# Gate and value products of a feed-forward block by seven half-size products (Strassen), in three parts instead of two

## The chip, the cores and the metric

The kernel runs on one core of one Trainium2 chip. The metric is the device time of one execution in microseconds (us). The core has five engines with a queue each: TensorE (PE in the profile; its weight loads are shown apart as PEld), VectorE (DVE), ScalarE (ACT), GpSimd (POOL) and SyncE (SP, which issues most DMAs here). Each engine works through its own queue in order, and an instruction that waits for a semaphore holds back all that stands behind it in that queue.

## The reference, cut to what matters

The kernel computes two transformer blocks on 512 tokens of width 1024, in fp32. The change lies in the feed-forward part of the first block only:

```python
h = rmsnorm(x, norm_ffn[layer])
x = x + (jax.nn.silu(h @ w_ffn_gate[layer]) * (h @ w_ffn_up[layer])) @ w_ffn_down[layer]
return rmsnorm(x, norm_final)          # D_MODEL = 1024, D_FF = 2816, SEQ = 512
```

`h @ w_ffn_gate` (gate) and `h @ w_ffn_up` (value) are two products of 512x1024 by 1024x2816. Everything before and after (an NSA and a GLA mixer before; MLA, sliding-window, FoX and again MLA layers after) is computed by code that the change leaves as it was.

## The kernel before, in words

Every fp32 operand of a matmul is split into two fp32r parts, high and low, by `split_into` (L213): ACT copies the source to the high part, DVE subtracts the high part from the source to get the low part. `mm3` (L270) then takes three matmuls for each pair of operands: high by high, low by high, high by low. Weights come by `wload` (L228): a raw tile `wr` of 128x1024 (pool `wraw`, 3 buffers) is filled by a DMA from SP's queue, and is then split into a pair `wh`, `wl` (pool `wpool`, 6 buffers of each).

The activations lie transposed, features on partitions, in `Ah` and `Al` (8 chunks of 128 features by 512 tokens). They are written by `to_feat` at the end of the stage before (`merge`), one block of 128 tokens at a time.

`ffn` (L866) works in two parts (`FF_PART` = 11 of the 22 chunks of 128 hidden units). In each part it goes over the chunks two at a time. For each chunk there are 24 matmuls of 512 columns for the gate (8 feature chunks by three) into one PSUM bank and 24 for the value into another. `silu2` (L284: a Tanh on ACT and a scalar_tensor_tensor on DVE), a multiply on DVE (L891) and a split (L892) leave the hidden chunk in `hdh`, `hdl`. The very first pair of chunks runs as two halves of 256 tokens, so that it can start before the last token blocks are there. At the end of a part `out_proj` (L395) multiplies the hidden chunks by the rows of `w_ffn_down`: for each of two halves of 512 output columns and four blocks of 128 tokens, 33 matmuls of 512 columns, and an epilogue that adds the result to the residual `X` (L896). After the last part, the epilogue also normalises each block (L900 to L905) and turns it round with `to_feat`.

The order of the instructions on each engine is not written out by hand. The tile framework's scheduler sets it when the program is built, from the order of the code, its own estimate of durations, and the buffers that the pools give out; on the chip the order is then fixed.

Of the kernel before, what the change touches and what calls it, by code (L numbers as in the profile page):

```python
# [29 lines left out]
GLA_LEVELS = (32, 16, 8, 4, 2, 1)  # L30
D_FF = 2816
FF_CHUNKS = D_FF // 128
FF_PART = FF_CHUNKS // 2

COL_Q = 0
COL_KV = 512
# [91 lines left out]
class Net:  # L128
# [210 lines left out]
    def after(self, later, earlier, how=mybir.DependencyClass.NoSync):  # L339
        self.tc.add_manual_dep(later, earlier.name, mybir.DependencyInfo(how, mybir.DependencyReason.DATA), reason="order")  # L340
# [489 lines left out]
    def merge(self, w, rooms, early, oa, ob, spare):  # L830
        nc, a, tc = self.nc, self.a, self.tc
        with ExitStack() as c1:
# [30 lines left out]

            self.out_proj(a["w_out"][0], Split([(0, KD, *mg)]), epilogue)

    def ffn(self):  # L866
        nc, a, tc = self.nc, self.a, self.tc
        with ExitStack() as c1:
            f1 = c1.enter_context(tc.tile_pool(name="f1", bufs=1))
            f2 = c1.enter_context(tc.tile_pool(name="f2", bufs=2))  # L870
            hd = [f1.tile([128, FF_PART, S], F32R, name=n) for n in ("hdh", "hdl")]
# [4 lines left out]
            for part in range(2):  # L876
                for m0 in range(0, FF_PART, 2):
                    n = min(2, FF_PART - m0) * 128
                    col = (part * FF_PART + m0) * 128
                    wgs, wus = self.w_cols(wg, col, n), self.w_cols(wu, col, n)  # L880
                    for t in range(n // 128):
                        halves = 2 if part == 0 and m0 == 0 else 1
                        for hf in range(halves):
                            tok = slice(hf * S // halves, (hf + 1) * S // halves)
                            pg, pu = self.pj(), self.pj()
                            pg, pu = pg[:, 0:S // halves], pu[:, 0:S // halves]
                            self.proj_feat(pg, wgs[t], self.act, tok=tok)
                            self.proj_feat(pu, wus[t], self.act, tok=tok)
                            s = f2.tile([128, S], F32, name="fs")[:, 0:S // halves]
                            self.silu2(s, pg)  # L890
                            nc.vector.tensor_tensor(out=s, in0=s, in1=pu, op=ALU.mult)  # L891
                            self.split_into(hd[0][:, m0 + t, tok], hd[1][:, m0 + t, tok], s)  # L892
# [432 lines left out]
```

## Time and profile before

| | |
|---|---|
| median of 3 runs | 1878.99 us (1877.96 to 1880.93) |
| the profiled execution | 1878.37 us, of which span 1876.6 us |
| PE busy | 1830.0 us, 98% of the span |
| DVE, ACT, POOL busy | 1149.9 us (61%), 873.6 us (47%), 156.7 us (8%) |
| mean granted TensorE clock | 0.996 of full speed |

The feed-forward block takes from about 477 to 860 us of the span. Its matmuls on the first pair of chunks end at 502, the first part's gate and value products at 602.5, its down products at 663. A matmul's busy time in the trace is longer than the distance from one matmul to the next, since they are pipelined: cost is read from start to start. The same holds in a smaller measure for DVE and ACT.

### The profile page before, as it was taken

What the parts mean: (1) busy time and instruction counts of PE and PEld (TensorE: products, weight loads), DVE (VectorE), ACT (ScalarE), POOL (GpSimd) and SP (SyncE); (2) the same over time, 40 slices, a digit from 0 to 9 for tenths busy, and PEclk for the clock granted to TensorE, in tenths of its full rate; (3) what the DMA queues carried; (4) which work ended last, traced back from release to release, by engine and by line L of the source; (5) the groups of instructions that cost most, each with busy time, mean ns of one, the idle gap of its engine ahead of it and who ended that gap; (6) DMA issues with size and microseconds to landing.
All of it is one profiled execution on the core that took longest, in us unless ns stands there. A gap on an engine that the chain in (4) does not pass through costs nothing.

```text
span 1876.6 us, 26623 instructions
## 1 busy us (share of the span) xinstructions
PE 1830.0 (98%) x9843; PEld 1491.2 (79%) x9843; DVE 1149.9 (61%) x2954; ACT 873.6 (47%) x1970; POOL 156.7 (8%) x213
## 2 busy tenths in 40 slices
PE   7999899999999999999999999999999999999997
PEld 6877687678888888889877788877888887988775
DVE  5564387754533243336878675566776666787866
ACT  4543246743322132224667535463566564366651
POOL 2211200000000000002000010251000000200001
PEclk9999899999999999999999999999999999999999
DMA  7322042042333143214221133221422322232111
GB/s 217 79 57 57 15 126 62 18 135 90 113 99 87 62 135 93 81 54 135 54 65 56 46 110 96 68 66 38 113 70 55 90 68 79 76 87 58 46 57 45
DMA packets 200781, 148.09 MB, mean 79 GB/s; under 512 B 8797, under 2 KB 178570, under 8 KB 200650
## 3 DMA queue, kind: packets, MB, share of 16 engines
q1 hardware_dynamic: 198858, 140.97, 26.0%
q0 software_dynamic: 1792, 5.42, 0.9%
q8 instruction: 77, 1.26, 0.3%
q14 instruction: 54, 0.44, 0.1%
HBM read 144.27 MB, written 2.10 MB: 78 GB/s over the span
## 4 chain that ended last, share of the span: by engine, by line
PE 81%; DVE 3%; ACT 2%; issue 1%; POOL 0%; DMA 0%; POOLq 0%; DVEq 0%; ACTq 0%
PE pj L273 22%; PE pj L274 22%; PE pj L275 22%; PE o L348 4%; PE t L335 3%; PE s L309 1%; PE s L274 1%; PE s L273 1%; PE s L275 1%; PE s L310 1%; PE t L370 1%; ACT pt L205 1%; PE t L1178 1%; PE s L1278 1%; PE s L1277 1%
## 5 line engine op out<-in xcount | busy, mean ns | idle before, releaser
L214 ACT ACTIVATE wh<-wr 128x1024 fp32r<-128x1024 f32 (+9 forms) x390 | 280.4, 749 | 461.1 <-PE pj L274 270.4
L215 DVE TENSOR_TENSOR wl<-wr,wh 128x1024 fp32r<-128x1024 f32 (+9 forms) x390 | 322.2, 849 | 225.4 <-ACT wh L214 223.0
L273 PE MATMUL pj<-Ah,wh 128*128 128x512 f32 (+1 forms) x1120 | 435.2, 389 | 1.3 <-DVE k4l L215 0.8
L274 PE MATMUL pj<-Al,wh 128*128 128x512 f32 (+1 forms) x1120 | 434.0, 388 | 0.0
L275 PE MATMUL pj<-Ah,wl 128*128 128x512 f32 (+1 forms) x1120 | 433.6, 388 | 0.0
L273 PEld LDWEIGHTS pj<-Ah,wh 128*128 128x128 f32 x1120 | 210.8, 188 | 45.4 <-PE s L275 1.6
L275 PEld LDWEIGHTS pj<-Ah,wl 128*128 128x128 f32 x1120 | 210.8, 188 | 44.3 <-issue 1.5
L274 PEld LDWEIGHTS pj<-Al,wh 128*128 128x128 f32 x1120 | 210.8, 188 | 42.4 <-issue 0.8
L273 PE MATMUL pj<-wh,Ah 128*128 128x512 f32 (+5 forms) x640 | 217.8, 341 | 4.7 <-ACT Ah L214 4.6
L274 PE MATMUL pj<-wl,Ah 128*128 128x512 f32 (+5 forms) x640 | 215.9, 338 | 0.0
L275 PE MATMUL pj<-wh,Al 128*128 128x512 f32 (+5 forms) x640 | 213.4, 338 | 2.0 <-DVE Al L215 1.9
L325 ACT ACTIVATE sp<-sp,nm 128x128 f32<-128x128 f32 (+3 forms) x256 | 142.7, 559 | 68.0 <-DVE nm L324 65.8
L205 ACT ACTIVATE pt<-t 128x512 f32<-128x512 f32 (+3 forms) x288 | 114.9, 445 | 114.4 <-PE t L335 74.8
L322 DVE CUSTOM_DVE_ANT_0 sp<-s,c_causal 128x128 f32<-128x128 f32 (+3 forms) x256 | 121.0, 486 | 62.8 <-PE s L275 23.5
L273 PEld LDWEIGHTS pj<-wh,Ah 128*128 128x128 f32 x640 | 120.5, 188 | 19.5 <-ACT Ah L214 7.1
L275 PEld LDWEIGHTS pj<-wh,Al 128*128 128x128 f32 x640 | 120.2, 188 | 14.0 <-DVE Al L215 3.0
L274 PEld LDWEIGHTS pj<-wl,Ah 128*128 128x128 f32 x640 | 120.7, 189 | 10.8 <-issue 0.2
L335 PE MATMUL t<-ident,sp 128*128 128x128 f32 x640 | 107.9, 277 | 4.9 <-ACT pt L205 4.8
L335 PEld LDWEIGHTS t<-ident,sp 128*128 128x128 f32 x640 | 77.3, 140 | 30.4 <-ACT pt L205 11.5
L329 DVE TENSOR_SCALAR sp<-sp,rc 128x128 f32<-128x128 f32 (+3 forms) x256 | 96.6, 383 | 5.0
L275 PE MATMUL pj<-wh,hdl 128*128 128x512 f32 x176 | 68.3, 389 | 0.0
L274 PE MATMUL pj<-wl,hdh 128*128 128x512 f32 x176 | 68.3, 390 | 0.0
(417 smaller groups left out, 2827.2 us busy)
## 6 DMA issues: line engine op xcount, KB each, us to landing
wr<-in_w_in_dram SPq DMA_DIRECT2D x34, 512.0 KB, 3.8
wr<-in_fox_w_in_dram SPq DMA_DIRECT2D x30, 512.0 KB, 4.2
wr<-in_w_ffn_gate_dram SPq DMA_DIRECT2D x22, 512.0 KB, 3.9
wr<-in_w_ffn_up_dram SPq DMA_DIRECT2D x22, 512.0 KB, 3.9
wr<-in_w_ffn_down_dram SPq DMA_DIRECT2D x20, 512.0 KB, 3.7
wr<-in_swa_w_in_dram SPq DMA_DIRECT2D x20, 512.0 KB, 4.3
wr<-in_mla_w_in_dram SPq DMA_DIRECT2D x16, 512.0 KB, 4.4
wr<-in_mla_w_out_dram SPq DMA_DIRECT2D x16, 512.0 KB, 3.8
```

What stands on the lines that cost most here:

```text
L205: return self.nc.scalar.activation(out, in_, AF.Copy, scale=1.0 if scale is None else scale)
L214: self.nc.scalar.activation(h, src, AF.Copy)
L215: self.nc.vector.tensor_tensor(out=l, in0=src, in1=h.bitcast(F32), op=ALU.subtract)
L273: self.nc.tensor.matmul(ps, lhsT=ah, rhs=bh, start=i == 0, stop=False)
L274: self.nc.tensor.matmul(ps, lhsT=ah, rhs=bl, start=False, stop=False)
L275: self.nc.tensor.matmul(ps, lhsT=al, rhs=bh, start=False, stop=i == n - 1)
L309: self.nc.tensor.matmul(ps, lhsT=q, rhs=kh, start=True, stop=False)
L322: nc.vector.tensor_tensor_reduce(out=v, in0=ps, in1=self.causal[:, S - n:S], scale=1.0, scalar=LOWEST, op0=ALU.add, op1=ALU.max, accum_out ...
L325: nc.scalar.activation(v, v, AF.Exp, bias=nm[:, g], accum_out=sm[:, g])
L329: nc.vector.tensor_scalar(v, v, rc[:, g], None, ALU.mult)
L335: nc.tensor.transpose(ps[:, (b - j) * 128:(b - j + 1) * 128], sp[:, POFF[b] + j * 128:POFF[b] + j * 128 + 128], self.ident)
L348: mm = self.nc.tensor.matmul(po[64 * i:64 * i + 64, j * 128:S], lhsT=value(j, i), rhs=pt[:, TOFF[j]:TOFF[j] + (NB - j) * 128], start=first ...
```

## The change

The first pair of chunks stays as it was, except that only its first chunk is run in halves. For the other 20 chunks, two chunks (256 hidden units) are taken together. The weights of such a pair are a 1024x256 matrix, cut into four blocks of 512x128 (b11, b21, b12, b22); the activations are cut into halves by feature and by token (a11, a12, a22, and a21). Gate and value each become one "group" of seven products (a Strassen-Winograd scheme): four sums of the activation blocks are made once (`half_sums`: s1 to s4), four sums of the weight blocks for each group on POOL (`sub`, in place in the raw tiles), and each of the seven products is 4 feature chunks by three matmuls of 256 columns, 84 matmuls in all. A bank `a` keeps adding up: it holds the first product, is copied out by ACT (`kept`), takes the second on top, is copied again, and so on. DVE adds the copies to other banks for the four quarters of the result.

A group needs four weight pairs instead of two: w0 (the raw first tile), w1 (half of the raw second tile), and, once POOL has made the sums, w3 (first tile) and w2 (second tile). The code interleaves the groups by generators: the first two products of a group, then the last two of the group before, then the middle three. The three parts have 8, 8 and 6 chunks, so the down product runs three times, with 24, 24 and 18 matmuls per block. The second raw tile comes from a pool of its own (`fr`, 2 buffers).

```diff
-FF_PART = FF_CHUNKS // 2
+FF_PARTS = (8, 8, 6)
...
+    def half_sums(self, pool, room):
...
+        for eng, f, k, tok in ((nc.vector, f11, lo, t0), (nc.gpsimd, f22, hi, t1), (nc.vector, f21, lo, t1), (nc.gpsimd, f12, hi, t0)):
+            eng.tensor_tensor(out=f, in0=q(self.Ah, k, tok).bitcast(F32), in1=q(self.Al, k, tok).bitcast(F32), op=ALU.add)
+        nc.gpsimd.tensor_tensor(out=f22, in0=f21, in1=f22, op=ALU.add)
+        nc.vector.tensor_tensor(out=f21, in0=f11, in1=f21, op=ALU.subtract)
+        nc.vector.tensor_tensor(out=f11, in0=f22, in1=f11, op=ALU.subtract)
+        nc.gpsimd.tensor_tensor(out=f12, in0=f12, in1=f11, op=ALU.subtract)
...
+    def halves_product(self, pool, raws, sums, w, n0, out):
+        nc = self.nc
+        v0 = self.wload(w, 0, KD, (n0, 128))
+        v1 = self.wload(w, 0, KD, (n0 + 128, 128), pool=raws)
+        b11, b21, b12, b22 = v0[:, 0:4], v0[:, 4:8], v1[:, 0:4], v1[:, 4:8]
+        w0 = self.wtile(KD, 128)
+        self.split_into(*w0, v0)
+        w1 = self.wtile(4, 128)
+        self.split_into(*w1, b22)
+        sub = lambda o, x, y, op=ALU.subtract: nc.gpsimd.tensor_tensor(out=o, in0=x, in1=y, op=op)
+        sub(b22, b22, b12)
+        sub(b12, b12, b11)
+        sub(b11, b11, b22, ALU.add)
+        sub(b21, b21, b11)
+        w3 = self.wtile(KD, 128)
+        self.split_into(*w3, v0)
+        w2 = self.wtile(KD, 128)
+        self.split_into(*w2, v1)
...
+        a, b, c = self.pj()[:, 0:256], self.pst()[:, 0:256], self.pss()[:, 0:256]
+        product(a, w0, 0, "a11", first=True)
+        p1 = kept(a)
+        product(b, w0, 4, "a12", first=True, last=True)
+        out(0, 0, p1, b)
+        yield
+        product(a, w3, 0, "s2")
+        u2 = kept(a)
+        product(c, w2, 0, "s1", first=True)
+        product(a, w2, 4, "s3")
+        u3 = kept(a)
+        out(1, 1, u3, c)
+        yield
+        product(c, w1, 0, "s4", last=True)
+        out(1, 0, u2, c)
+        product(a, w3, 4, "a22", last=True)
+        out(0, 1, a, None)
+        yield
...
+                    for group in pair(m, (k0 + m) * 128):
+                        next(group)
+                        if before is not None:
+                            next(before)
+                            next(before, None)
+                            if after is not None:
+                                after()
+                                after = None
+                        next(group)
+                        before = group
```

How the built programs stand is shown at three places, all in the middle of the stage (before: first part; after: second part). On DVE before, `wl` is the low part of a weight tile, `fs` a gate tile, `pj` a PSUM bank:

```order
L215 TENSOR_TENSOR wl_5003<-wr_5000,wh_5002 128x1024 [waits DMAHW1_49,PE_49,Activation_49]
L286 SCALAR_TENSOR_TENSOR fs_4858<-fs_4858,pj_4808 128x512 [waits Activation_49]
L891 TENSOR_TENSOR fs_4858<-fs_4858,pj_4809 128x512 [waits DVE_49,PE_49]
L215 TENSOR_TENSOR wl_5009<-wr_5006,wh_5008 128x1024 [waits DMAHW2_49,Activation_49]
L215 TENSOR_TENSOR hdl_4340<-fs_4858,hdh_4339 128x512 [waits Activation_49]
```

One period of DVE after, from the batch of four weight splits of one group to the next batch. 6231 and 6235 are w3 and w2 of a value group, made from the raw tiles 6214 and 6216; 6348 and 6352 are w0 and w1 of the group behind it, from 6343 and 6345; `fg` and `fu` are gate and value tiles, `part` a copy of bank `a`:

```order
L215 TENSOR_TENSOR wl_6231<-wr_6214,wh_6230 128x1024 [waits Activation_49]
L215 TENSOR_TENSOR wl_6235<-wr_6216,wh_6234 128x1024 [waits Activation_49]
L215 TENSOR_TENSOR wl_6348<-wr_6343,wh_6347 128x1024 [waits DMAHW4_49,Activation_49]
L215 TENSOR_TENSOR wl_6352<-wr_6345,wh_6351 128x512 [waits DMAHW7_49,Activation_49]
L1001 SCALAR_TENSOR_TENSOR fg_6083<-fu_6294,fg_6083 128x512 [waits Activation_49]
L1001 SCALAR_TENSOR_TENSOR fg_6084<-fu_6297,fg_6084 128x512 [waits Activation_49]
L993 TENSOR_TENSOR fu_6213<-part_6338,s_6240 128x256 [waits DVE_49,Activation_49]
L993 TENSOR_TENSOR fg_6341<-part_6382,t_6368 128x256 [waits PE_49,Activation_49]
L993 TENSOR_TENSOR fu_6213<-part_6312,s_6240 128x256 [waits PE_49]
L961 TENSOR_TENSOR fg_6084<-fg_6084,fu_6213 128x512 [waits DVE_49]
L215 TENSOR_TENSOR wl_6360<-wr_6343,wh_6359 128x1024 [waits Activation_49]
```

In place of one weight split at a time, with a wait for PE between them, DVE now has four in a row, and two groups are mixed in them: w3 and w2 of one group stand ahead of w0 and w1 of the next.

On ACT before, the high parts:

```order
L214 ACTIVATE wh_5002<-wr_5000 128x1024 [waits DMAHW1_49,PE_49]
L285 ACTIVATE fs_4858<-pj_4808 128x512 [waits PE_49,Activation_49]
L214 ACTIVATE wh_5008<-wr_5006 128x1024 [waits DMAHW2_49,PE_49]
L214 ACTIVATE hdh_4339<-fs_4858 128x512 [waits DVE_49]
L214 ACTIVATE wh_5014<-wr_5012 128x1024 [waits DMAHW3_49,PE_49]
```

and after, in the same period as DVE's above:

```order
L214 ACTIVATE wh_6230<-wr_6214 128x1024 [waits Pool_49]
L214 ACTIVATE wh_6234<-wr_6216 128x1024 [waits Activation_49]
L214 ACTIVATE wh_6347<-wr_6343 128x1024 [waits DMAHW4_49,PE_49,Activation_49]
L214 ACTIVATE wh_6351<-wr_6345 128x512 [waits DMAHW7_49,PE_49]
L205 ACTIVATE fg_6083<-pj_6109 128x256 [waits PE_49]
L205 ACTIVATE part_6312<-pj_6238 128x256 [waits PE_49]
L1000 ACTIVATE fu_6294<-fg_6083 128x512 [waits Activation_49]
L1000 ACTIVATE fu_6297<-fg_6084 128x512 [waits DVE_49]
L205 ACTIVATE part_6338<-pj_6238 128x256 [waits PE_49]
```

The first high part of a batch now waits for POOL, and behind it in the queue stand the high parts that the next group starts with.

On POOL before, there is nothing between the last block of the stage before and the final normalisation (these rows follow each other):

```order
L377 TENSOR_SCALAR rms_4310<-ss1_4308 128x1 [waits DVE_49]
L225 TENSOR_TENSOR rmso_4312<-rms_4310,mhalf_84 128x1 [waits Pool_49]
L222 DMA gf_4342<-in_norm_final_dram 128x1024 [waits DMAHW3_49,DMAHW4_49,DVE_49,DMAHW5_49,PE_49,Activation_49]
L377 TENSOR_SCALAR rms_6563<-ss1_6561 128x1 [waits DVE_49]
L225 TENSOR_TENSOR rmso_6565<-rms_6563,mhalf_84 128x1 [waits Pool_49]
```

and after, four sums for each of 20 groups (here the groups of the raw tiles 6085 and 6087, and the first of 6214 and 6216):

```order
L907 TENSOR_TENSOR wr_6087<-wr_6087 128x512 [waits DMAHW3_49,DVE_49]
L907 TENSOR_TENSOR wr_6087<-wr_6087,wr_6085 128x512 [waits DMAHW0_49,Pool_49]
L907 TENSOR_TENSOR wr_6085<-wr_6085,wr_6087 128x512 [waits Pool_49]
L907 TENSOR_TENSOR wr_6085<-wr_6085 128x512 [waits Pool_49]
L907 TENSOR_TENSOR wr_6216<-wr_6216 128x512 [waits DMAHW5_49,DVE_49]
```

The first of the four waits for DVE (the split of w1 from the same raw tile), and each of the others for the one ahead of it.

## Rows read from the trace of the kernel before

**Rows 1.** The page: span, and busy time of each engine.
```profile
span 1876.6 us, 26623 instructions
PE 1830.0 (98%) x9843; PEld 1491.2 (79%) x9843; DVE 1149.9 (61%) x2954; ACT 873.6 (47%) x1970; POOL 156.7 (8%) x213
```
**Rows 2.** Windows: stretch, length, busy PE, PEld, DVE, ACT, POOL; clock, DMA share, GB/s.
```profile
500.00:602.00 102.00, 102.00 (x450) 83.14 (x449) 40.07 (x47) 28.68 (x38) 0.00 (x0) 1.00 0.33 95
```
**Rows 3.** Waits of PE from 475 to 870: us in total, times, longest.
```profile
PE t L370 <- DVE Al L215: 0.4, 1, 0.4
```
**Rows 4.** Timeline of PE: start, duration, line, tiles, shape.
```profile
496.08 0.28 PE L273 MATMUL pj<-Ah,wh 128*128 128x256 f32 x1
...
498.93 0.28 PE L273 MATMUL pj<-Ah,wh 128*128 128x256 f32 x1
...
502.14 0.40 PE L273 MATMUL pj<-Ah,wh 128*128 128x512 f32 x1
...
602.52 0.40 PE L273 MATMUL pj<-wh,hdh 128*128 128x512 f32 x1
```
**Rows 5.** Groups by line and shape, 475 to 870: count, busy, mean ns.
```profile
L215 DVE TENSOR_TENSOR wl<-wr,wh 128x1024 fp32r<-128x1024 f32 x61 | 74.7, 1226 | 98.8 <-ACT wh L214 98.2
L891 DVE TENSOR_TENSOR fs<-fs,pj 128x512 f32<-128x512 f32 x20 | 13.7, 687 | 55.6 <-PE pj L275 55.6
L215 DVE TENSOR_TENSOR hdl<-fs,hdh 128x512 fp32r<-128x512 f32 x20 | 13.7, 685 | 0.2
L215 DVE TENSOR_TENSOR wl<-wr,wh 128x512 fp32r<-128x512 f32 x4 | 2.7, 685 | 0.0
L214 ACT ACTIVATE wh<-wr 128x1024 fp32r<-128x1024 f32 x60 | 63.6, 1061 | 216.6 <-PE pj L274 148.4 <-PE pj L275 43.6 <-DMA wr<-in_w_ffn_down_dram 8.3
```
**Rows 6.** Timeline of ACT, then DVE, in the stage: weight splits and their followers.
```profile
518.84 1.06 ACT L214 ACTIVATE wh<-wr 128x1024 fp32r<-128x1024 f32 x1 [4.00 <-PE pj L274]
519.81 0.58 ACT L285 ACTIVATE fs<-pj 128x512 f32<-128x512 f32 x1
...
519.93 1.23 DVE L215 TENSOR_TENSOR wl<-wr,wh 128x1024 fp32r<-128x1024 f32 x1 [3.76 <-ACT wh L214]
...
525.50 1.22 DVE L215 TENSOR_TENSOR wl<-wr,wh 128x1024 fp32r<-128x1024 f32 x1 [0.18 <-ACT wh L214]
526.65 0.69 DVE L215 TENSOR_TENSOR hdl<-fs,hdh 128x512 fp32r<-128x512 f32 x1
```
**Rows 7.** POOL's two-input operations, by line: count, duration ns min/median/max.
```profile
L419 POOL TENSOR_TENSOR xg<-X,nm x2: 2385/2392/2398, 12.3 to 19.5; 128x1024 f32<-128x1024 f32 x2
L621 POOL TENSOR_TENSOR f<-gk,f x24: 460/572/1483, 64.9 to 210.1; 128x128 f32<-128x128 f32 x24
L612 POOL TENSOR_TENSOR f<-cum x24: 612/625/1432, 60.9 to 208.0; 128x256 f32<-128x256 f32 x24
```
**Rows 8.** Timeline of POOL, then DVE, 11 to 23 us.
```profile
12.32 2.40 POOL L419 TENSOR_TENSOR xg<-X,nm 128x1024 f32<-128x1024 f32 x1 [5.98 <-DMA X<-in_x_dram]
...
17.58 0.28 POOL L377 TENSOR_SCALAR rms<-ss 128x1 f32<-128x1 f32 x1
17.94 0.55 POOL L225 TENSOR_TENSOR rmso<-rms,mhalf 128x1 f32<-128x1 f32 x1
...
11.82 0.68 DVE L215 TENSOR_TENSOR Al<-t,Ah 128x512 fp32r<-128x512 f32 x1
12.43 2.92 DVE L215 TENSOR_TENSOR wl<-wr,wh 128x592 fp32r<-128x592 f32 x1
```
**Rows 9.** Timeline of POOL, then DVE, near 65 us.
```profile
64.87 1.48 POOL L621 TENSOR_TENSOR f<-gk,f 128x128 f32<-128x128 f32 x1 [1.81 <-ACT wh L214]
...
64.82 1.22 DVE L215 TENSOR_TENSOR wl<-wr,wh 128x1024 fp32r<-128x1024 f32 x1
```
**Rows 10.** Timeline of DVE, then POOL, near 1162 us.
```profile
1161.69 0.18 DVE L1165 RECIPROCAL sum<-sum 128x4 f32<-128x4 f32 x1
...
1162.05 0.94 POOL L1169 TENSOR_SCALAR sp<-sp,sum 128x256 f32<-128x256 f32 x1 [3.31 <-DVE sum L1165]
```

More of the change, by code (lines that the diff above doesn't have):

```diff
@@ L225, in power_half, with wload @@
         self.nc.gpsimd.tensor_tensor(out=out, in0=var, in1=self.mhalf[:, 0:n], op=ALU.pow)
-    def wload(self, w, k0, kc, *ranges):
+    def wload(self, w, k0, kc, *ranges, pool=None):
         n = sum(r[1] for r in ranges)
-        t = self.wraw.tile([128, 1024], F32, name="wr")
+        t = (self.wraw if pool is None else pool).tile([128, 1024], F32, name="wr")
         v = t[:, 0:kc * n].rearrange("p (k n) -> p k n", n=n)
@@ L864, in merge, with splits @@
             self.out_proj(a["w_out"][0], Split([(0, KD, *mg)]), epilogue)
+    def half_sums(self, pool, room):
+        nc = self.nc
+        lo, hi, t0, t1 = slice(0, 4), slice(4, 8), slice(0, 256), slice(256, 512)
+        q = lambda t, k, tok: t[:, k, tok]
+        f11, f21, f12, f22 = (room.tile([128, 4, 256], F32, name=n) for n in ("f11", "f21", "f12", "f22"))
+        for eng, f, k, tok in ((nc.vector, f11, lo, t0), (nc.gpsimd, f22, hi, t1), (nc.vector, f21, lo, t1), (nc.gpsimd, f12, hi, t0)):
[4 more added lines that the diff above has]
+        nc.gpsimd.tensor_tensor(out=f12, in0=f12, in1=f11, op=ALU.subtract)
+        out = {"a11": (q(self.Ah, lo, t0), q(self.Al, lo, t0)), "a12": (q(self.Ah, hi, t0), q(self.Al, hi, t0)), "a22": (q(self.Ah, hi, t1), q(self.Al, hi, t1))}
+        def splits():
+            for n, src in (("s2", f11), ("s3", f21), ("s1", f22), ("s4", f12)):
+                if n == "s1":
+                    h, l = q(self.Ah, lo, t1), q(self.Al, lo, t1)
+                else:
+                    h, l = (pool.tile([128, 4, 256], F32R, name=n + u) for u in "hl")
+                self.split_into(h, l, src)
+                out[n] = (h, l)
+            return out
+        return splits
@@ new lines, in halves_product, with product, kept @@
+    def halves_product(self, pool, raws, sums, w, n0, out):
+        nc = self.nc
+        v0 = self.wload(w, 0, KD, (n0, 128))
[14 more added lines that the diff above has]
+        self.split_into(*w2, v1)
+        def product(ps, wt, k0, name, first=False, last=False):
+            sh, sl = sums[name]
+            for k in range(4):
+                (ah, al), (bh, bl) = (wt[0][:, k0 + k], wt[1][:, k0 + k]), (sh[:, k], sl[:, k])
+                for i, (x, y) in enumerate(((ah, bh), (ah, bl), (al, bh))):
+                    nc.tensor.matmul(ps, lhsT=x, rhs=y, start=first and k == 0 and i == 0, stop=last and k == 3 and i == 2, skip_group_check=True)
+        def kept(ps):
+            t = pool.tile([128, 256], F32, name="part", bufs=4)
+            self.acopy(t, ps)
+            return t
+        a, b, c = self.pj()[:, 0:256], self.pst()[:, 0:256], self.pss()[:, 0:256]
[16 more added lines that the diff above has]
+        yield
@@ L869, in ffn @@
             f1 = c1.enter_context(tc.tile_pool(name="f1", bufs=1))
-            f2 = c1.enter_context(tc.tile_pool(name="f2", bufs=2))
-            hd = [f1.tile([128, FF_PART, S], F32R, name=n) for n in ("hdh", "hdl")]
+            raws = c1.enter_context(tc.tile_pool(name="fr", bufs=2))
+            most = max(FF_PARTS)
+            hd = [f1.tile([128, most, S], F32R, name=n) for n in ("hdh", "hdl")]
             st = f1.tile([128, NB, 2], F32, name="fss")
@@ L875, in ffn, with hidden @@
             wg, wu = a["w_ffn_gate"][0], a["w_ffn_up"][0]
[L876 to L892, printed above, removed]
+            def hidden(m, s, u, tok=slice(0, S)):
+                nc.vector.tensor_tensor(out=s, in0=s, in1=u, op=ALU.mult)
+                self.split_into(hd[0][:, m, tok], hd[1][:, m, tok], s)
@@ new lines, in ffn @@
+            with tc.tile_pool(name="f0", bufs=1) as f0:
+                splits = self.half_sums(f1, f0)
+                wgs, wus = self.w_cols(wg, 0), self.w_cols(wu, 0)
+                for t in range(2):
+                    halves = 2 - t
+                    for hf in range(halves):
+                        n = S // halves
+                        tok = slice(hf * n, (hf + 1) * n)
+                        pg, pu = self.pj()[:, 0:n], self.pj()[:, 0:n]
+                        self.proj_feat(pg, wgs[t], self.act, tok=tok)
+                        self.proj_feat(pu, wus[t], self.act, tok=tok)
+                        s = f0.tile([128, S], F32, name="fg", bufs=2)[:, 0:n]
+                        self.silu2(s, pg)
+                        hidden(t, s, pu, tok)
+                sums = splits()
@@ new lines, in ffn, with pair, add, out @@
+            f2 = c1.enter_context(tc.tile_pool(name="f2", bufs=2))
+            def pair(m, col):
+                g = [f2.tile([128, S], F32, name="fg", bufs=4) for _ in range(2)]
+                u = []
+                def add(tiles):
+                    def out(t, half, x, y):
+                        o = tiles[t][:, half * 256:half * 256 + 256]
+                        if y is None:
+                            self.acopy(o, x)
+                        else:
+                            nc.vector.tensor_tensor(out=o, in0=x, in1=y, op=ALU.add)
+                    return out
+                def gates():
+                    yield from self.halves_product(f2, raws, sums, wg, col, add(g))
+                    for t in g:
+                        th = f2.tile([128, S], F32, name="fu", bufs=3)
+                        nc.scalar.activation(th, t, AF.Tanh, scale=0.5)
+                        nc.vector.scalar_tensor_tensor(out=t, in0=th, scalar=1.0, in1=t, op0=ALU.add, op1=ALU.mult)
+                def ups():
+                    u.extend(f2.tile([128, S], F32, name="fu", bufs=3) for _ in range(2))
+                    yield from self.halves_product(f2, raws, sums, wu, col, add(u))
+                    for t in range(2):
+                        hidden(m + t, g[t], u[t])
+                return gates(), ups()
@@ L894, in epilogue, with down @@
+            def down(part, k0, n):
                 def epilogue(b, half, ps):
@@ L896, in epilogue @@
                     nc.vector.scalar_tensor_tensor(out=xv, in0=ps, scalar=0.5, in1=xv, op0=ALU.mult, op1=ALU.add)
-                    if part == 0:
+                    if part < len(FF_PARTS) - 1:
                         return
@@ L906, in epilogue @@
                         self.to_feat(self.X[:, b], b)
-                self.out_proj(a["w_ffn_down"][0], Split([(0, FF_PART, *hd)]), epilogue, kc=FF_PART, k0=part * FF_PART)
+                self.out_proj(a["w_ffn_down"][0], Split([(0, n, *hd)]), epilogue, kc=n, k0=k0)
+            k0, before, after = 0, None, None
+            for part, n in enumerate(FF_PARTS):
+                for m in range(0, n, 2):
+                    if part == 0 and m == 0:
+                        continue
+                    for group in pair(m, (k0 + m) * 128):
[8 more added lines that the diff above has]
+                        before = group
+                after = lambda part=part, k0=k0, n=n: down(part, k0, n)
+                k0 += n
+            next(before)
+            next(before, None)
+            after()
     def finish_layer(self, i, w, og, last):
```

## The prediction

> **What bounds the kernel now.** I read the page first: PE is busy for 98% of the span, the next engine, DVE, for 61% [rows 1]. Then the windows: from 500 to 602 us, the first part's gate and value products, PE is busy all the time at full clock, DVE for 40 of 102 us, ACT for 29, POOL not at all [rows 2]. Then PE's waits: the longest in the whole feed-forward stage is 0.4 us [rows 3]. So PE alone sets the time there, and what it costs is the number of matmuls times the distance from start to start. For 512 columns that is (602.52 - 502.14) / 432 = 0.2324 us (9 chunks of 48 matmuls), for 256 columns (498.93 - 496.08) / 24 = 0.1188 us [rows 4]: half the columns cost 51%.
>
> **What PE saves.** The 20 chunks had 960 matmuls of 512 columns, 223.1 us. They now have 20 groups of 84 of 256 columns: 1680 x 0.1188 = 199.6 us, 9.98 us a group. In the first pair, 96 matmuls of 256 become 48 of 512: -0.2 us. The down products keep 528 matmuls. If PE stays the bound, that is -23.7 us.
>
> **Whether the other engines can feed it.** Per group DVE has three splits of 1024 columns and one of 512, 3 x 1.23 + 0.69 = 4.4 us, plus three additions of 256 columns and two to four operations of 512; ACT has the high parts and four copies. Both stay below 10 us, and a count of busy time would call the change covered. But the order rows show a closed loop. ACT's high part of w3 waits for POOL's fourth sum. On DVE the low parts of w3 and w2 of this group stand ahead of those of w0 and w1 of the next. POOL's first sum for the next group waits for that w1, and the next group's w3 waits for POOL's fourth. Every group goes once round this loop, whatever PE does. I time it from the start of the high part of w3:
>
> - DVE starts on the low part 1.09 us later (518.84 to 519.93) and starts the next operation 1.15 us after a split of 1024 (525.50 to 526.65) [rows 6]. Low parts of w3, w2, w0, w1 start at 1.09, 2.24, 3.39 and 4.54; the last one, of 512 columns, takes 0.69 [rows 5] and ends at 5.23. ACT, with 0.97 us from start to start [rows 6], keeps ahead.
> - POOL starts 0.18 us behind DVE (1161.87 to 1162.05) [rows 10], at 5.41.
> - A sum of two tiles of 128x512 on POOL isn't in the trace. The same operation took 2.39 us for 128x1024 and at least 0.46 for 128x128 [rows 7]; the straight line gives 1.29. The lower end is 0.92, from 0.61 for 128x256 (there the second input is one column repeated) and that 0.46; the upper end is 1.34, with the 0.28 of an operation on one column [rows 8] as the fixed part ((2.39 - 0.28) / 2 + 0.28). I take 1.29, since both inputs are whole tiles as in the 1024 row. Four of them with 0.08 between (17.86 to 17.94) [rows 8] are 5.40: done at 10.81.
>
> So the loop takes 10.81 us with nothing in its way, 0.83 more than PE's 9.98. The cover that the sums seem to have, a whole group of PE time, is not there.
>
> [...] The rows allow 0.92 to 1.34. [...]
>
> **POOL and DVE hold each other up.** At 12.43 DVE's split of 592 columns took 2.92 us, although 512 take 0.69: POOL's multiplication ran from 12.32 to 14.72, and DVE ended 0.63 later [rows 5, 8]. The other way round, POOL's 128x128 took 1.48 instead of 0.46 when DVE's split had started 0.05 ahead of it [rows 7, 9]. Whoever is second waits for the whole of the other. In the loop, while POOL makes its sums, DVE has two-input operations on SBUF tiles: two scalar_tensor_tensor in the period in which a gate group ends, and the product and two low parts of the hidden chunks where a value group ends (L961, then L215 twice). I let them take turns. DVE's first follows 0.61 after w1's start (11.82 to 12.43 for 512 columns) [rows 8], at 5.15, and ends at 5.83, so POOL starts at 5.83 instead of 5.41.
>
> - Gate: sum to 7.12, DVE to 7.80, sum to 9.09, two more with 0.08 ahead of each: 11.83.
> - Value: sum to 7.13, DVE to 7.81, sum to 9.10, DVE to 9.79, sum to 11.08, sum to 12.45.
>
> Mean 12.14 us, 2.16 more than PE needs. Bounds: 0.83 more with no such clashes; none at all, if a sum takes 0.92 and nothing clashes (loop 9.33). From above, about 3.2, if a clash costs one more wait in each period.
>
> **How often.** Parts have 6, 8 and 6 groups. Behind a down product the sums of the first group are done, so the loop is paid 5 + 7 + 5 = 17 times: 17 x 2.16 = 36.7 us. At each start of a part PE has two products (2.85 us) in hand while ACT copies bank a and makes the high parts of w3 and w2, 0.97 apart; the order puts two matmuls of w2 behind two of w3, so PE stands about 0.8 us, three times: 2.4.
>
> **The rest.** Half sums: POOL has three operations of 2.39 and eight sums of 1.29 to make after the last token block, 17.5 us, and DVE some eleven two-input operations of 1.15 at the same time, 12.7; PE has about 16 us of the first pair and 5.7 of first products (48 matmuls) to cover them. Were they to exclude each other fully, some 30 - 22 = 8 us would show; half of that and a little, 5 (0 to 10). The third down product adds eight additions to X on DVE and no matmul; the row splits of each down product now meet the last group's batch. One split (1.15) each, 3 us (0 to 6). Weight traffic is the same; SP's loads wait for buffers that come free a group ahead.
>
> **Sum**, against the profiled execution's own 1878.4 us (span 1876.6 [rows 1] and 1.8 around it; the median is 1879.0): -23.7 + 36.7 + 2.4 + 5 + 3 = +23.4: 1902 us. Its own range, with the last two terms at either end and 0.3 us on the period: 1889 to 1915.
>
> **Rivals.**
> - *The loop turns, but cheaper.* Either the clashes do not add up, since POOL slips between DVE's operations (10.81): -23.7 + 14.1 + 10.4 = +0.8, 1879; or a sum takes 0.92 and they do (10.66): 1877. For it: DVE's two-input operations fill only 1.4 to 2 us of a period. Against it: both rows of a clash show the full wait. 16%.
> - *PE stays the bound, faster.* Place: the queue of the high parts on ACT. If a sum takes under 1.08 us and nothing clashes, w3 is ready before PE asks, and only the opening is paid: -23.7 + 5 = 1860. It decides at a period of 9.98; the whole change breaks even at 9.98 + 13.3 / 17 = 10.76, with clashes a sum of 0.95. For it: the 0.61 row; PE's order has other products to fill in. Against it: the 2.39 row. 19%.
> - *A second wait inside the group.* Bank a is copied by ACT between products that PE adds to it; where the copy stands behind a Tanh or a high part, PE stands too. At 1 us for each of 17 periods that does not fall into the loop's slack: 1919. Against it: 12 to 20 matmuls lie between. 10%.
> - That the matmuls do not fall to 1680 is ruled out by the order.
>
> **Chances.** The forecast has 55%. What a measurement can tell from no change is about 0.2%, 3.8 us. Faster: the 19% and a quarter of the first rival, 23%. Same: half of that rival, 8%. Slower: the rest, 69%. The range runs from the PE-bound rival to the upper end of the forecast, 1859 to 1916; beyond lie the second wait and the worst of the opening.
>
> **What would show it.** In the profile after: POOL's sums on wr at 1.29 us or up to 2 where DVE is in the way; in the middle of a part PE idle some 2 us per group, waiting for ACT wh (w3) released by POOL; groups 12 us apart; POOL busy for about half of the stage; 256-column matmuls still 0.119 apart. A PE without gaps in the groups, or sums under 1 us, would make the forecast wrong; sums held up by DVE in no row would cut it to no change.

## The result, and the profile after

The changed kernel takes 1895.29 us (median of 4 runs, 1895.15 to 1895.97) against 1878.94 us: ratio 1.0086, 95% interval 1.0071 to 1.0101. The prediction was 1902 us (1859 to 1916).

The page of the changed kernel, answering to [rows 1], with the head of its chain of waits:

```profile
span 1893.3 us, 28314 instructions
...
PE 1821.4 (96%) x10515; PEld 1511.5 (80%) x10515; DVE 1253.8 (66%) x3065; ACT 933.6 (49%) x2090; POOL 285.7 (15%) x297
...
PE 51%; issue 12%; POOL 7%; DVE 2%; ACT 1%; POOLq 0%; DVEq 0%; ACTq 0%
PE pj L273 13%; PE pj L274 13%; PE pj L275 13%; POOL wr L907 6%; PE o L348 3%; PE t L335 3%; PE s L274 1%; PE s L273 1%; PE s L275 1%; PE t L370 1%; PE t L1318 1%; PE s L1418 1%; PE s L1417 1%; PE o L1273 1%; PE s L309 0%
```

POOL, busy for 15% of the span, has 7% of the chain, nearly all of it in the sums (L907). The window over the second part's groups, answering to [rows 2] (same columns):

```profile
629.00:727.00 98.00, 89.64 (x683) 84.02 (x682) 69.58 (x82) 48.81 (x81) 47.28 (x32) 1.00 0.32 95
```

PE, full in [rows 2], has gaps; every other engine is idle for a quarter of the time or more. Such a picture asks for a closed chain of waits. The two largest waits of POOL and ACT from 640 to 720 us (total, times, longest):

```profile
POOL wr L907 <- DVE wl L215: 38.3, 7, 5.6
ACT wh L214 <- POOL wr L907: 21.3, 7, 3.2
```

One round of it, in the timelines of POOL (first four rows; a row is one batch, the four sums of a group), ACT, DVE and PE, and then the durations (ns, least, median, most) of the gate's scalar_tensor_tensor (L1001) and, from 583 us on, of the low parts of the hidden chunks:

```profile
629.42 5.40 POOL L907 TENSOR_TENSOR wr<-wr 128x512 f32<-128x512 f32 x4 [49.68 <-DVE wl L215]
640.36 6.11 POOL L907 TENSOR_TENSOR wr<-wr 128x512 f32<-128x512 f32 x4 [5.53 <-DVE wl L215]
652.09 6.45 POOL L907 TENSOR_TENSOR wr<-wr 128x512 f32<-128x512 f32 x4 [5.62 <-DVE wl L215]
663.83 6.11 POOL L907 TENSOR_TENSOR wr<-wr 128x512 f32<-128x512 f32 x4 [5.30 <-DVE wl L215]
...
658.57 3.48 ACT L214 ACTIVATE wh<-wr 128x1024 fp32r<-128x1024 f32 x4 [3.21 <-POOL wr L907]
669.98 2.95 ACT L214 ACTIVATE wh<-wr 128x1024 fp32r<-128x1024 f32 x3 [2.93 <-POOL wr L907]
...
652.53 3.48 DVE L215 TENSOR_TENSOR hdl<-fg,hdh 128x512 fp32r<-128x512 f32 x2
659.65 4.10 DVE L215 TENSOR_TENSOR wl<-wr,wh 128x1024 fp32r<-128x1024 f32 x4 [0.55 <-ACT wh L214]
663.67 2.38 DVE L1001 SCALAR_TENSOR_TENSOR fg<-fu,fg 128x512 f32<-128x512 f32 x2
...
659.67 0.38 PE L922 MATMUL pj<-s2h,wh 128*128 128x256 f32 x1 [0.80 <-ACT wh L214]
660.62 0.39 PE L922 MATMUL s<-Ah,wh 128*128 128x256 f32 x1 [0.45 <-ACT wh L214]
...
L1001 DVE SCALAR_TENSOR_TENSOR fg<-fu,fg x20: 681/1020/1782, 526.2 to 825.4; 128x512 f32<-128x512 f32 x20
L215 DVE TENSOR_TENSOR hdl<-fg,hdh x16: 683/1772/1785, 586.3 to 837.8; 128x512 fp32r<-128x512 f32 x16
```

At 658.57 ACT starts the high part of w3, 0.03 us after POOL's last sum. DVE's four low parts begin 1.08 later and end at 663.75; POOL starts 0.08 behind, and ACT starts the next group's w3 at 669.98. From batch to batch (the period) it is 11.73 and 11.74 us; PE's 84 matmuls need 9.98. The first batch of a part meets nothing on DVE and takes 5.40, four sums of 1.29 with 0.08 between. Later ones take 6.11 where the two scalar_tensor_tensor of a gate fall into them, 6.45 where the hidden chunks do. Those DVE operations take longer too: of a gate's two the first, which starts ahead of the batch, takes 0.68 and the second 1.78, and each low part of a hidden chunk 1.78.

### The profile page after: what moved, and what is told of

Same layout as the page of the kernel before. It is cut to its first block, busy times and chain, and to the rows that moved or that the text cites. A ratio compares the mean times of both kernels' runs of the same rounds, so it can differ in the third digit from the quotient of the medians.

```text
span 1893.3 us, 28314 instructions
## 1 busy us (share of the span) xinstructions
PE 1821.4 (96%) x10515; PEld 1511.5 (80%) x10515; DVE 1253.8 (66%) x3065; ACT 933.6 (49%) x2090; POOL 285.7 (15%) x297
## 4 chain that ended last, share of the span: by engine, by line
PE 51%; issue 12%; POOL 7%; DVE 2%; ACT 1%; POOLq 0%; DVEq 0%; ACTq 0%
PE pj L273 13%; PE pj L274 13%; PE pj L275 13%; POOL wr L907 6%; PE o L348 3%; PE t L335 3%; PE s L274 1%; PE s L273 1%; PE s L275 1%; PE t L370 1%; PE t L1318 1%; PE s L1418 1%; PE s L1417 1%; PE o L1273 1%; PE s L309 0%
## 5 line engine op out<-in xcount | busy, mean ns | idle before, releaser
L214 ACT ACTIVATE wh<-wr 128x1024 fp32r<-128x1024 f32 (+10 forms) x428 | 307.2, 758 | 329.6 <-PE pj L274 108.3
L215 DVE TENSOR_TENSOR wl<-wr,wh 128x1024 fp32r<-128x1024 f32 (+10 forms) x428 | 357.3, 865 | 156.2 <-ACT wh L214 152.8
L273 PE MATMUL pj<-Ah,wh 128*128 128x512 f32 (+1 forms) x784 | 306.3, 391 | 2.3 <-DVE fg L286 1.0
L274 PE MATMUL pj<-Al,wh 128*128 128x512 f32 (+1 forms) x784 | 305.1, 389 | 0.2 <-DVE Al L215 0.2
L275 PE MATMUL pj<-Ah,wl 128*128 128x512 f32 (+1 forms) x784 | 304.6, 389 | 0.0
L273 PEld LDWEIGHTS pj<-Ah,wh 128*128 128x128 f32 x784 | 147.6, 188 | 32.9 <-PE s L275 1.6
L275 PEld LDWEIGHTS pj<-Ah,wl 128*128 128x128 f32 x784 | 147.6, 188 | 30.5 <-issue 1.5
L274 PEld LDWEIGHTS pj<-Al,wh 128*128 128x128 f32 x784 | 147.6, 188 | 29.3 <-issue 0.8
L322 DVE CUSTOM_DVE_ANT_0 sp<-s,c_causal 128x128 f32<-128x128 f32 (+3 forms) x256 | 120.8, 486 | 63.0 <-PE s L275 23.5
L907 POOL TENSOR_TENSOR wr<-wr 128x512 f32<-128x512 f32 x80 | 119.3, 1491 | 202.7 <-DVE wl L215 198.1
L274 PEld LDWEIGHTS pj<-wl,Ah 128*128 128x128 f32 x640 | 120.7, 189 | 10.8 <-issue 0.2
```

Of the source, the lines that this page charges most:

```text
L214: self.nc.scalar.activation(h, src, AF.Copy)
L215: self.nc.vector.tensor_tensor(out=l, in0=src, in1=h.bitcast(F32), op=ALU.subtract)
L273: self.nc.tensor.matmul(ps, lhsT=ah, rhs=bh, start=i == 0, stop=False)
L274: self.nc.tensor.matmul(ps, lhsT=ah, rhs=bl, start=False, stop=False)
L275: self.nc.tensor.matmul(ps, lhsT=al, rhs=bh, start=False, stop=i == n - 1)
L322: nc.vector.tensor_tensor_reduce(out=v, in0=ps, in1=self.causal[:, S - n:S], scale=1.0, scalar=LOWEST, op0=ALU.add, op1=ALU.max, accum_out ...
```

## Experiments

The scheduler sets the order of the instructions anew for each edit, and in the traces it is never quite the old one (in e1, for instance, PE takes product s4 in the midst of s2). So a difference of two medians is the edit together with its order; what the batches and the waits show is safer.

**Is it the round?**

```diff
-        sub(b22, b22, b12)
-        sub(b12, b12, b11)
-        sub(b11, b11, b22, ALU.add)
-        sub(b21, b21, b11)
```

> The changed kernel without POOL's four sums of the weight blocks: w3 and w2 are split from the raw tiles, so the output is another one; loads, splits, matmuls and copies are all there. Loop theory (each group waits for the round low parts on DVE, four sums on POOL, high part on ACT, 11.73 us in the trace after, against 9.98 us of matmuls): the loop is gone, 17 x 1.75 = 29.8 us and the three starts of a part (2.4) come back, 1895.3 - 32 = 1863 us, and PE has no gap over 0.3 us in the middle of a part. Rival (the order of the seven products holds PE: bank a has to be copied by ACT between products that are added to it, or ACT is late with its high parts anyway): little comes back, 1885 to 1895.

Measured: 1872.85 us, ratio 0.9969 (0.9957 to 0.9980). Of the 32 us 22 came back: the sums hold the kernel, but something stands behind them. In the second and third part groups are still 10.8 to 10.9 us apart (read, here and below, from the first matmul of product s4 of one group to that of the next). Timelines of ACT and PE of this run:

```profile
643.94 1.06 ACT L214 ACTIVATE wh<-wr 128x1024 fp32r<-128x1024 f32 x1 [0.28 <-PE pj L918]
...
644.97 0.39 PE L918 MATMUL s<-Ah,wl 128*128 128x256 f32 x1 [0.71 <-DVE wl L215]
```

The high part of w2 waits for PE, its low part comes after that, and PE waits for the low part. What PE holds can be one of the six shared weight buffers; e6 below takes w1 out of them.

**Is it the meeting of POOL and DVE?** The gate's scalar_tensor_tensor is taken out, a hidden chunk is only copied, and the low parts of the hidden chunks are zeroed once, at the opening:

```diff
+                nc.vector.memset(hd[1][:, 2:most].bitcast(F32), 0.0)
...
-                        nc.vector.scalar_tensor_tensor(out=t, in0=th, scalar=1.0, in1=t, op0=ALU.add, op1=ALU.mult)
...
-                        hidden(m + t, g[t], u[t])
+                        nc.scalar.activation(hd[0][:, m + t], u[t], AF.Copy)
```

> The sums stay on POOL, but DVE loses the operations with two SBUF inputs that fall into their time: the scalar_tensor_tensor of a gate group, the product and the low parts of the hidden chunks (the low parts are zeroed once, so the output differs). Theory (DVE and POOL hold each other up where both read two SBUF tiles, which costs 0.71 us in a gate period and 1.04 in a value period): batches of four sums take 5.40 us everywhere, the period falls from 11.73 to 5.18 + 0.08 + 5.40 + 0.05 = 10.7, 17 x 1.0 = 17 us less, 1878 us. Rival (the longer batches have another reason, or the time sits on ACT): batches stay at 6.1 to 6.4 us and the time at 1890 to 1895. Should PE be the bound once the clashes are gone, it would be 1863.

Measured: 1885.37 us, ratio 1.0034 (1.0021 to 1.0047). Timelines of POOL, ACT, DVE:

```profile
696.58 5.38 POOL L907 TENSOR_TENSOR wr<-wr 128x512 f32<-128x512 f32 x4 [5.59 <-DVE wl L215]
707.56 5.39 POOL L907 TENSOR_TENSOR wr<-wr 128x512 f32<-128x512 f32 x4 [5.60 <-DVE wl L215]
...
702.00 3.48 ACT L214 ACTIVATE wh<-wr 128x1024 fp32r<-128x1024 f32 x4 [2.22 <-POOL wr L907]
...
703.05 0.42 DVE L994 TENSOR_TENSOR fg<-part,s 128x256 f32<-128x256 f32 x1 [1.98 <-PE s L922]
703.39 4.09 DVE L215 TENSOR_TENSOR wl<-wr,wh 128x1024 fp32r<-128x1024 f32 x4
```

This is the bare round: batches of 5.4 as expected, so the meetings are what made them longer. The additions that take an input from PSUM meet nothing: the one at 711.64 takes 0.42 beside a batch of 5.39, and the one at 703.05 also 0.42 with POOL idle. The period is 10.98, 0.28 over the expectation, since an addition from PSUM (0.34 to the next start) stands ahead of the first low part. Meetings cost 0.75 us a period, by the forecast's count of periods 17 x 0.75 = 12.7 us. 9.9 came back: the zeroing, which runs on DVE, delays the opening, where PE now waits 3.8 and 3.4 us for low parts of `Al` (at most 0.4 in the changed kernel).

**Has POOL room?**

```diff
+        sub(b21, b21, b11)
```

> A fifth operation of 128x512 on POOL behind the four sums of each group (the last sum once more, so the output differs). Loop theory: POOL is busy for 48% of the stage, and still each group is longer by one sum and its gap, 1.29 + 0.08 = 1.37 us, 17 times: +23 us, 1919 us, period 13.1; a further clash with DVE would make it 1925. Rival (POOL has slack in a group, the waits on it are an effect of something else being late): no change, 1895.

Measured: 1921.53 us, ratio 1.0225 (1.0210 to 1.0241): 26.2 us more. POOL's batches, now of five sums:

```profile
675.21 7.45 POOL L907 TENSOR_TENSOR wr<-wr 128x512 f32<-128x512 f32 x5 [5.63 <-DVE wl L215]
688.55 7.13 POOL L907 TENSOR_TENSOR wr<-wr 128x512 f32<-128x512 f32 x5 [5.90 <-DVE wl L215]
```

In the second part they come 12.4 to 14.4 us apart, mean 13.4, in place of 11.73. POOL was busy for 48% of this stretch (46.73 us from 629 to 727), and the added sum still lengthened the round by its whole price and more. That it is 3 us over the expectation can be the clock (granted 0.95 from 629 to 727 us, 1.00 in the changed kernel) or more meetings; that stays open.

**Sums on DVE.**

```diff
-        sub = lambda o, x, y, op=ALU.subtract: nc.gpsimd.tensor_tensor(out=o, in0=x, in1=y, op=op)
+        sub = lambda o, x, y, op=ALU.subtract: nc.vector.tensor_tensor(out=o, in0=x, in1=y, op=op)
```

> The four sums on DVE instead of POOL, nothing else. Loop theory: the round is then 5.2 us of splits and four sums of 0.60 to 0.69 us, about 8 us, under PE's 9.98, and nothing meets on POOL; but DVE gets 4.4 (splits) + 2.6 (sums) + 1.2 (additions from PSUM) + 2.1 (hidden chunks, mean of gate and value) = 10.2 us of work per group by its durations, about 9.3 by its starts. If the starts count, PE is the bound: 1863 to 1868 us, faster than the kernel before. If the durations count or the order on DVE is bad, DVE is the bound at 10.2 to 10.7: 1869 to 1878. Rival (the order of the products holds PE): 1885 to 1895.

Measured: 1874.47 us, ratio 0.9974 (0.9963 to 0.9985): faster than both kernels, and the best of the complete ones here. In the timeline of DVE a sum costs 0.60 from start to start, and nothing holds it up:

```profile
688.32 0.68 DVE L907 TENSOR_TENSOR wr<-wr 128x512 f32<-128x512 f32 x1
688.92 0.41 DVE L993 TENSOR_TENSOR fg<-part,s 128x256 f32<-128x256 f32 x1
```

It isn't the 1863 to 1868 of a PE without gaps: toward the end of a part groups come 10.8 to 11.3 apart, at its start 7.3 to 10.0.

**Weight buffers.** In e5, e6 and e7 w1 gets two buffers of its own (and `fsq` shares the tiles `fu`, for room):

```diff
-        w1 = self.wtile(4, 128)
+        w1 = [self.w1pool.tile([128, 4, 128], F32R, name=n) for n in ("w1h", "w1l")]
```

> The changed kernel, with w1 (the half-size pair) taken from a pool of its own with 2 buffers instead of from the 6 shared ones, so that the 6 serve w0, w2, w3 alone. Without the sums (e1) the groups still came 10.85 us apart, with ACT waiting for PE to free a weight buffer. Theory (two bounds one behind the other: the round through POOL at 11.73 us, the 6 weight buffers at 10.85): the buffers are not what ends last here, the period stays at 11.7 and the time at 1893 to 1896. Rival (the buffers hold the round itself, since ACT's high parts wait for them): the period falls towards 10.8, 1878 to 1882.

Measured: 1905.56 us, ratio 1.0141 (1.0128 to 1.0155), outside both expectations. With another pool the scheduler set another order: in the first part PE stands 10.0 us once, and two periods of each later part are 13.7 to 15.3 us. It decides neither for the theory nor for the rival, as buffers and order changed together.

> Both at once: no sums of the weight blocks (w2 and w3 are split from raw tiles, so the output is another one) and w1 in a pool of its own. Theory of two bounds: nothing is left above PE's 84 x 0.1188 = 9.98 us a group, 17 x 0.87 = 15 us less than the 1872.9 of e1: 1858 us. Rival (the 10.85 is not the buffers but the copies of bank a or the order of the products): the period stays at 10.8, 1871 to 1873.

Measured: 1858.86 us, ratio 0.9892 (0.9877 to 0.9907). The time is what the theory expected, 14 us less than e1. PE's longest item of waiting in the whole stage is this, the rest are 0.4 or less:

```profile
PE pj L918 <- ACT part L205: 2.0, 2, 1.3
```

That is what seven products with their splits take when nothing but PE bounds them. But as in e5 the order changed with the buffers, so that the six buffers are the second bound is likely and not shown.

> The four sums on DVE (as in e4, whose later groups came 10.8 to 11.3 us apart, the earlier ones of a part 9.9) and w1 in a pool of its own; nothing is left out. Theory of two bounds: e4's last groups of a part ran into the weight buffers; with them out of the way the period is 9.98 to 10.2 (DVE's own work), some 9 periods x 0.8 = 7 us less than the 1874.5 of e4: 1867 us. Rival (DVE is the bound in e4): no change, 1873 to 1876.

Measured: 1879.34 us, ratio 1.0002 (0.9993 to 1.0011). Worse than e4, with another order again: one wait of 6.3 us at the opening, then periods of 10.3 and 11.3 in turn.

**Opening the round while the sums stay on POOL.** The next group's weights are fetched, split and summed ahead of this group's w3 and w2 in the code, and w1 has a pool of its own:

```diff
+        v0, v1, w0, w1 = ready.pop()
+        fetch()
         w3 = self.wtile(KD, 128)
```

> The sums stay on POOL. The weights of the next group are loaded, w0 and w1 split and the four sums started ahead of this group's splits of w3 and w2 in the code (one group ahead), and w1 has a pool of its own; nothing is left out. Loop theory: low parts of w3 and w2 no longer stand between a group's sums and the next ones, POOL has a whole period for its 5.4 to 6.5 us, PE is the bound: periods 9.98, 1895.3 - 29.8 - 2.4 = 1863 us, faster than the kernel before by 16 us. If the clashes of POOL and DVE alone cost PE time (DVE's low parts come later by 0.7 to 1.0 us a group, but need not be waited for): up to 1875. Rival (loads come too late for two groups ahead, or w1's two buffers hold the order): 1878 to 1890.

Measured: 1905.58 us, ratio 1.0141 (1.0127 to 1.0155). The expectation failed, and the timelines show that the edit didn't do what I meant: in the second part w1's low part still stands behind three others, and POOL's batch behind it.

```profile
680.56 3.49 DVE L216 TENSOR_TENSOR wl<-wr,wh 128x1024 fp32r<-128x1024 f32 x3
683.97 0.68 DVE L216 TENSOR_TENSOR w1l<-wr,w1h 128x512 fp32r<-128x512 f32 x1
...
684.73 6.44 POOL L908 TENSOR_TENSOR wr<-wr 128x512 f32<-128x512 f32 x4 [5.94 <-DVE w1l L216]
```

So e9 ties the order down: the splits of w3 and w2 are issued behind that of the next group's w1. For room w1 has three buffers and the weights of the final normalisation go to a raw tile.

```diff
+        with ExitStack() as late:
+            for ins in ready[0][4] if ready else ():
+                late.enter_context(self.tc.issue_after(ins.ins))
...
```

> As e8 (the next group's weights loaded and its w0, w1 split ahead; sums on POOL; nothing left out), but now the splits of w3 and w2 are tied behind the split of the next group's w1 on ACT and DVE, which in e8's trace still stood behind them, and w1 has 3 buffers (the final norm's weights go to a raw tile). In the order of DVE each group is now w1 of the next group, w3, w2, w0 of the one after. Loop theory: the sums of group n+1 run while PE works on group n; the round takes two groups, about 6 us for each; PE is the bound at 9.98 us a group, as in e6: 1859 to 1866 us, 13 to 20 us faster than the kernel before, although POOL and DVE meet as often as in the changed kernel (sums of 1.5 us, hidden chunks' low parts of 1.4 us). Rival (meetings cost PE time of themselves, by low parts that come late): periods of 10.5 to 11, 1870 to 1880. Rival (loads two groups ahead come too late): 1885 or more, with ACT waiting for DMAs.

Measured: 1909.35 us, ratio 1.0162 (1.0148 to 1.0176). The order is now the one intended, and it is slower still. POOL, then DVE, then one of ACT's waits from 640 to 735 us:

```profile
676.60 7.98 POOL L908 TENSOR_TENSOR wr<-wr 128x512 f32<-128x512 f32 x4 [7.05 <-DVE w1l L906]
688.79 8.36 POOL L908 TENSOR_TENSOR wr<-wr 128x512 f32<-128x512 f32 x4 [4.21 <-DVE w1l L906]
...
676.78 6.65 DVE L216 TENSOR_TENSOR wl<-wr,wh 128x1024 fp32r<-128x1024 f32 x3 [0.26 <-ACT wh L215]
688.03 0.68 DVE L906 TENSOR_TENSOR w1l<-wr,w1h 128x512 fp32r<-128x512 f32 x1
688.63 0.68 DVE L970 TENSOR_TENSOR fg<-fg,fu 128x512 f32<-128x512 f32 x1
689.24 6.76 DVE L216 TENSOR_TENSOR wl<-wr,wh 128x1024 fp32r<-128x1024 f32 x3
...
ACT w1h L906 <- PE s L933: 11.1, 4, 5.2
```

The sums no longer wait for the low parts of w3 and w2; they run beside them. A batch alone takes 5.40, three low parts alone 3.41 (680.56 to 683.97 in e8), 8.81 one after the other; side by side they take 7.98. A tenth is gained by overlap. (The batch at 688.79 takes 8.36, as it meets what is left of a multiply as well.) And the order has a wait of its own: ACT's high part of w1 waits for PE, 11.1 us in four waits, and POOL's batch stands behind it. So e9 shows that this order loses; it doesn't show that every order with the sums on POOL does. Last, e9 with the sums on DVE:

> e9 with the four sums on DVE instead of POOL; nothing is left out. In e9 the order no longer held the sums back, and the groups still came 12 us apart: POOL's four sums took 8.4 us and DVE's three low parts of 1024 columns beside them 6.7 instead of 3.5. Theory (operations of POOL and DVE with two SBUF inputs shut each other out, so that 5.4 us of sums and DVE's 5 to 6 us of such work add up past 9.98 in any order): without POOL, DVE has by its starts 4.05 (splits) + 2.4 (four sums of 0.60) + 1.0 (three additions of 0.34) + 1.2 or 2.4 (hidden chunks) = 9.2 us a group, PE is the bound again: periods 10.0 to 10.3, 1860 to 1868 us. Rival (what held e9 is its order: w1 waiting for a PE product, copies of bank a late on ACT): periods stay at 11.5 to 12.5, 1895 to 1909.

Measured: 1879.65 us, ratio 1.0004 (0.9995 to 1.0013): 30 us less than e9, which is what the sums on POOL cost in that order; but 12 to 20 us over the expectation, so the rival has its part. Periods inside a part are 9.4 to 12.3, mean 11.0. PE's largest wait of the whole stage, and one instance in the timelines of ACT and PE:

```profile
PE pj L933 <- ACT part L206: 7.9, 11, 1.2
...
684.31 2.94 ACT L215 ACTIVATE wh<-wr 128x1024 fp32r<-128x1024 f32 x3
687.15 0.61 ACT L1018 ACTIVATE fu<-fg 128x512 f32<-128x512 f32 x1
687.67 0.63 ACT L206 ACTIVATE part<-pj 128x256 f32<-128x256 f32 x2
...
688.08 0.38 PE L933 MATMUL pj<-Ah,wh 128*128 128x256 f32 x1 [1.17 <-ACT part L206]
```

The copy of bank a stands on ACT behind three high parts and a Tanh, and PE stands with it.

**The small terms.** First the changed kernel with the opening's sums and their splits left out:

```diff
+        for n, src in (("s2", "a11"), ("s3", "a12"), ("s4", "a22")):
+            out[n] = out[src]
```

> The changed kernel without the four sums of the activation blocks at the opening (no adds and no splits there; s1 to s4 are existing quarters of Ah and Al, so the output is another one). The prediction gave the opening 5 us (0 to 10). Theory (PE waits 2.4 us for a low part and 2.1 for a high part in the first groups, and holds are shifted to the first period of the round): 5 us less, 1890 us. Rival (the round would have held the first groups anyway): 0 to 1 us less, 1894 to 1895. Rival (POOL's and DVE's clashes at the opening cost more than seen): 10 us less, 1885.

Measured: 1892.14 us, ratio 1.0068 (1.0053 to 1.0084): the opening costs 3.2 us. The wait of 2.4 us for a low part there is gone, that of 2.1 for a high part too; in their place PE waits 2.2 for the stage before.

Then the kernel before in three parts:

```diff
-            for part in range(2):
+            for part, size in enumerate(FF_PARTS):
```

> The kernel before with three parts (8, 8 and 6 chunks) instead of two of 11, its gate and value products as before, nothing else. The prediction gave the third down product and the row splits 3 us (0 to 6). Theory (the same matmuls in all, PE full over the downs but for one wait of up to 1.4 us): 0 to 2 us more, 1879 to 1881. Rival (each change between products and down costs a wait of its own): 4 us or more, 1883.

Measured: 1878.79 us, ratio 0.9999 (0.9990 to 1.0008): a third down product costs nothing.

## Why the prediction was right, step by step

The sign, the place and the mechanism held. That the sum is only 7 us too high is in part luck: the round cost 16 us less than forecast, and against it stand 11 us in the first and last groups that the forecast didn't see.

| term | predicted | measured | from |
|---|---|---|---|
| PE's matmuls | -23.7 | -23.5 | an estimate: e6 (-20.3) less the 3.2 of the opening |
| the round | +36.7 (17 x 2.16) | +20.7 (12 x 1.73) | the 12 periods of 11.1 to 11.9 us in the trace, less 9.98 each |
| starts of a part | +2.4 (three) | +4.3 (two) | 2 x (66.74 - 64.58), see below |
| first and last groups of the stage | in the two terms above | +11.4 | rest: after less e6 is 36.4 |
| opening (half sums) | +5 | +3.2 | e10 |
| third down, row splits | +3 | -0.3 | e11 (no row splits meet a batch there) |
| sum | +23.4 | +15.8 | measured: +16.4 |

- *PE bounds the kernel before, and 84 matmuls of 256 columns take 9.98 us.* Right: e6 is 20.3 us faster than the kernel before, with the 3.2 of the half sums in it.
- *The closed loop.* Right, by each of its waits, and by e1, e2 and e3. w3's start to w1's end: 5.18 against 5.23; POOL starts 0.08 behind DVE, not 0.18 [rows 10]. A sum takes 1.29, as the line through [rows 7] said.
- *POOL and DVE hold each other up.* The step that was mis-sized. Forecast: 1.02 (gate) and 1.64 (value) over an undisturbed batch; measured: 0.71 and 1.05. I took the full turn of [rows 8] for each meeting. Two meetings of 0.60 in a gate batch cost 0.71, not 1.20, so about a quarter of a us of each turn is hidden. The forecast's own rows had shown it: POOL ended 0.31 behind DVE where its operation alone takes 0.46 [rows 7, 9].
- *How often.* The count of 17 doesn't stand in the trace. The starts of s4 in the first part are 6.83, 10.02, 11.81, 11.10 and 11.88 us apart, in the second six times 11.6 to 11.8, in the third 11.83, 11.62, 11.85 and 13.79: 12 full rounds. The time that the table gives to the first and last groups lies mostly ahead of the first s4: from 505.07 to 526.87 us PE runs 112 matmuls of 256 columns, 13.3 us at 0.1188, in 21.8. That is 8.5 us, against 1.0 in e6, which has the half sums but no sums of weights. PE's two largest waits from 500 to 580 us, and a stretch shortly behind the wait of 2.4 (columns as in [rows 2]):

```profile
PE s L922 <- ACT wh L214: 3.4, 4, 2.1
PE pj L922 <- DVE wl L215: 2.4, 1, 2.4
510.75:514.16 3.41, 3.41 (x18) 3.41 (x17) 3.41 (x5) 0.63 (x1) 0.48 (x1) 0.50 0.64 180
```

  The longest of the first, 2.1 us, is for a high part that waits for POOL. In the stretch, 0.6 us behind the idle 2.4, TensorE's clock was granted at 0.50, and matmuls of 256 columns started 0.214 us apart (510.78 to 513.77, 14 steps): 18 stand there, where at 0.1188 it would be some 29. The forecast had nothing for the clock, and for such waits 0.8 us at each start of a part.
- *Starts of a part.* Too low: 0.8 us each against 2.2. From the first matmul of product s4 at 578.51 us to that at 645.25 it is 66.74 us for two groups and a down product, 2 x 9.98 + 192 x 0.2324 = 64.58 by [rows 4]. The round of the group at this passage is in it.
- *The rival "PE stays the bound" at 1860.* Its mechanism was incomplete. I had it decide at a period of 9.98; e1 shows a second bound at 10.85 right behind the first, by its waits the weight buffers. With cheaper sums alone it would have ended near e1's 1873.
- *The rival "a second wait inside the group".* It wasn't the changed kernel's fate (0.7 us of waits for copies in the whole stage), but it is real: it is PE's largest wait in e12, 7.9 us.
- *What I didn't see.* I told it as an order of waits that could be undone. e9 undid it and lost, in part to a ring of its own. By start distances ([rows 6], and 0.60 for 512 columns in e4) DVE has 3 x 1.15 + 0.60 of weight splits and 2 or 4 x 0.60 of hidden work with two SBUF inputs in each group, 5.25 or 6.45 us. With POOL's 5.40 that is 10.65 or 11.85, mean 11.25, if the two work strictly in turn. With the 0.83 that overlap saved in e9 it is about 10.4, an estimate: past PE's 9.98, but under the break-even of the prediction (10.76). So whether some order with the sums on POOL gains is open; of those tried (e5, e8, e9) none did.

What keeps e4 and e7 from e6's 1858.9 was only read from waits; an order with the sums on DVE, w1's own buffers and copies of bank a ahead of the high parts wasn't tried.

## What to carry to other kernels

When an edit moves work to an idle engine, look in the order for a ring of waits through it: its length (here 11.73 us), not anybody's busy share, is the price: a share of 48% was no room at all (one more sum cost 26.2 us in e3). Where POOL and DVE read two SBUF tiles each at the same time, count POOL's operations as if they ran on DVE: here it is nearly the sum of both that counts (7.98 us side by side, 8.81 in turn, e9). Look for the second bound just behind the first (10.85 behind 11.73, e1) before pricing what its removal gives. And count in the trace how often a cost is paid (12 full rounds, not 17), not in the code alone.

## What the runs showed of the hardware

- Side by side, POOL's four sums and DVE's three low parts took 7.98 us, against 8.81 in turn: sharing the work between the two gained 9% (e9).
- The same sum of 128x512 takes POOL 1.37 us from start to start and DVE 0.60, and moving it from the engine at 15% to the one at 66% made the kernel 1.1% faster (e4 against the changed kernel).
- One more buffer pool made the kernel 10 us slower (e5), with the same instructions: with an order that a scheduler sets, an edit of buffers is an edit of order.
